# Moving five layer-1 modulation pieces of a two-layer hybrid kernel from the first mixer into the first expert stage

## The chip, the core and the metric

The kernel runs on one core of one Trainium2 chip. The metric is the device time of one execution in microseconds (us). The core has five instruction streams that run beside each other: TensorE (PE, matmuls), VectorE (DVE), ScalarE (ACT), GpSimd (POOL) and SyncE (SP). SP's queue issues nearly all transfers from memory; the core's 16 DMA engines carry them out.

## What is computed

Two layers over 256 tokens of width 1024. Each layer computes a modulation vector from the conditioning vector, uses six slices of it (shift, scale and gate, once for the mixer and once for the experts), and ends in a mixture of 16 experts. Cut to what matters:

```python
for layer in range(2):
    mod = silu(c) @ ada_w[layer] + ada_b[layer]        # 1024 x 6144 weights
    shift1, scale1, gate1, shift2, scale2, gate2 = split(mod, 6)
    h = rmsnorm(x, norm_mix[layer]) * (1 + scale1) + shift1
    mix = attention_and_recurrence(h) if layer == 0 else fnet(h)
    x = x + gate1 * mix
    h2 = rmsnorm(x, norm_ffn[layer]) * (1 + scale2) + shift2
    x = x + gate2 * grouped_moe(h2)                    # 16 experts, 1024 -> 512 -> 1024
```

In the kernel `ada_w[layer]` is cut into 12 pieces `(l, j)` of 512 columns, 2 MB each. Pieces `(1, 0)` and `(1, 1)` are layer 1's first shift, `(1, 2)` and `(1, 3)` its first scale; both are read only after the experts of layer 0. `(1, 6)` is half of layer 1's second shift, read later still.

## The kernel before, in words

All weights flow through 16 slots of 1 MB (`NSLOT`), in one fixed order. `Stream.pump` (L114 to L130) issues the next half of a piece as soon as a slot is free; SP's queue then waits for the last reader of that slot. So the order of the stream and the moments at which slots are given back set when each transfer starts.

The work goes through these stages, with times of the profiled execution:

- up to about 140 us: modulation of the first mixer, its first projections, the forward recurrence;
- 140 to 182 us: the value projection (`vp`, eight steps of 12 matmuls) beside the backward recurrence on DVE, ACT and POOL;
- 182 to 252 us: attention (16 units: scores `s`, softmax, transposes `pt`, weighted sums `av`) with the output projection `mix` interleaved;
- 252 to 278 us: norm, router, ranks, the gathering of the first four experts' tokens `xg`;
- 278 to 492 us: the experts of layer 0, eight pairs; for each pair the matmuls `g`, `u` (L1054), `dn` (L1091), and scatter and gather matmuls between them;
- 492 to 575 us: the second mixer (FNet), norm and router;
- 575 us to the end: the experts of layer 1.

Eleven modulation pieces (`ADA`, L30) are worked into the first mixer as a side task. `ada_ve` (L365 to L389) sums a piece on DVE: one `tensor_scalar` and seven `scalar_tensor_tensor` of 128x512 into the buffer `gva`, then four tiny PE products with ones (L386) add over the partitions, and a small DVE addition writes `modc`. `ada_step` (pieces 2, 3 and 9 of the list, `ON_PE`) does a piece with 32 PE products (L333) instead. The side task goes on by so many steps at each step of the projections (`W_K`, `W_Q`, `W_G`, `W_V`, `W_A`, `W_P`). `ORDER` (L37) says where the pieces stand in the stream: each `a` is the next of `ADA`, the capitals are projection weights, `p` and `o` the output projection's.

The order on PE in the expert stages is the order of the code (`manual_schedule`); elsewhere a scheduler places instructions on each engine by priority and by its own estimates, and each engine then keeps that order strictly. `W.used(k)` and `W.done(i)` give a slot back.

Of the kernel before, what the change touches and what calls it, by code (L numbers as in the profile page):

```python
# [13 lines left out]
ALU = mybir.AluOpType  # L14
# [12 lines left out]
PRI = 50  # L27
LOW = 60

ADA = [(0, 4), (0, 5), (0, 6), (0, 7), (0, 8), (0, 9), (1, 0), (1, 2), (1, 1), (1, 3), (1, 6)]  # L30
ON_PE = (2, 3, 9)

FILL0 = [[(0, 10), (0, 11)], [(1, 4), (1, 5)], []]
FILL1 = [[(1, 10), (1, 11)], [], []]
A1_LATE = [(1, j) for j in (7, 8, 9, 10, 11)]

ORDER = 'aaQBaaGaaaVpoaaaa'  # L37

EK = 'vgvgvggv'
EQ = 'vggvggvv'  # L40
# [106 lines left out]
def hybrid_layers(  # L147
# [22 lines left out]
    ve, ac, te, gp = nc.vector, nc.scalar, nc.tensor, nc.gpsimd  # L170
# [11 lines left out]
    def wps(name="w"):  # L182
        return ps.tile([128, 512], F32, tag="w", name=name, bufs=3)

    def gps(name="g"):
        return ps.tile([128, 512], F32, tag="g", name=name, bufs=1)

    def buf(name, tag, size, bufs):
        return data.tile([128, size], F32, tag=tag, name=name, bufs=bufs)
# [23 lines left out]
    st = Stream(nc, slots, NSLOT)  # L213

    def ada_item(l, j):
        return st.chunk(("a", l, j), ada_w[l, j])
# [4 lines left out]
    def exp_items(l):  # L221
        order = [(n, p) for p in range(NE // 2) for n in "gud"]
        if l == 1:
            order[-6:] = [(n, p) for ns in ("gu", "d") for p in (6, 7) for n in ns]
        r = []
        for n, p in order:
            pair = [st.chunk((n, l, e), {"g": moe_g, "u": moe_u, "d": moe_d}[n][l, e], n == "d")
                    for e in (2 * p, 2 * p + 1)]
            if (l, n, p) == (1, "d", 7):

                r += [(c, a // 512, slice(a % 512, a % 512 + b - a)) for a, b in zip(CUTS, CUTS[1:]) for c in pair]
            else:
                r += [(c, i) for i in range(2) for c in pair]
        return r

    WQ, WK, WV, WXB, WGB = range(5)
# [12 lines left out]
    ones = cst[:, 128:256]  # L249
# [52 lines left out]
    ada_b = [cols[:, 94:142], cols[:, 142:190]]  # L302

    sc32 = const.tile([128, 8, 32], F32, name="sc32")
# [13 lines left out]
    modc = [const.tile([128, 48], F32, name=f"modc{l}") for l in range(2)]  # L318
# [49 lines left out]
    def ada_ve(l, j):  # L368

        W = st.get(("a", l, j))  # L370
        while not W.ready(0):
            yield
        r = buf("gva", "gva", 512, 1)
        with tc.high_priority(-LOW):
            ve.tensor_scalar(r, W[:, 0], sc32[:, 0, 0:1], None, op0=ALU.mult)
        yield
        for k in range(1, 8):
            while k == 4 and not W.ready(1):
                yield
            with tc.high_priority(-LOW):  # L380
                ve.scalar_tensor_tensor(r, W[:, k], sc32[:, k, 0:1], r, op0=ALU.mult, op1=ALU.add)  # L381
            W.used(k)
            yield
        p = gps("gv")
        for q in range(4):
            te.matmul(out=p[:, q:q + 1], lhsT=r[:, q * 128:(q + 1) * 128], rhs=ones[:, 0:1], start=True, stop=True)  # L386
        yield
        c4 = slice(4 * j, 4 * j + 4)
        ve.tensor_tensor(modc[l][:, c4], p[:, 0:4], ada_b[l][:, c4], op=ALU.add)  # L389
        yield  # L390

    def split(dst_h, src, dst_l, eng):
# [125 lines left out]
    def rows(p, w, nt, k):  # L518

        for t in range(nt):  # L520
            c = slice(t * 128, (t + 1) * 128)
            mm3(p[t], (hH[k][:, c], hL[k][:, c]), w, k == 0, k == 7)
# [35 lines left out]
    for g in range(2):  # L558
# [3 lines left out]
             "o": [st.chunk(("wo", 1), w_out[1])], "p": [st.chunk(("wo", 0), w_out[0])]}  # L562
    ada = iter(ADA)
    for c in ORDER:
        st.add(named[c] if c in named else [ada_item(*next(ada))])
# [37 lines left out]
    def gemm(W, step, on):  # L603

        w = {k: split_w(W[:, k], ENG[on[k]]) for k in range(2)}
        for k in range(8):
            if k + 2 < 8:
                w[k + 2] = split_w(W[:, k + 2], ENG[on[k + 2]])
                W.used(k + 2)
            step(w.pop(k), k)  # L610
            yield
# [92 lines left out]
    scan = [Task(r.scan()) for r in rec]  # L704
    side = Task(*[(ada_step if i in ON_PE else ada_ve)(*a) for i, a in enumerate(ADA)])
    for n, _ in enumerate(gemm(st.get(("win", WK)), lambda w, k: rows(kp, w, 4, k), EK)):
# [180 lines left out]
    def moe(l, xn, store):  # L887
# [5 lines left out]
        for kk in range(4):  # L893
            p = wps("tp")
            for i in range(4):
                k = 2 * kk + i // 2
                at = te.transpose(p[:, i * 128:(i + 1) * 128], xn[:, i % 2, k * 128:(k + 1) * 128], ident)
            for i in range(2):
                k = 2 * kk + i
# [10 lines left out]
        for k in range(8):  # L910
            q = slice(32 * (k % 4), 32 * (k % 4) + 32)
# [104 lines left out]
        def half(i):  # L1016
            return slice(64 * i, 64 * i + 64)
# [28 lines left out]
        def up(p, xg):  # L1046

            i0 = 2 * (p % 2)
            gu = [wps("g"), wps("u")]
            for n, q in zip("gu", gu):  # L1050
                W = [st.get((n, l, 2 * p + i)) for i in range(2)]
                for k in range(8):
                    for i in range(2):
                        te.matmul(out=q[half(i), :], lhsT=xg[:, k, half(i0 + i)], rhs=W[i][:, k],  # L1054
                                  start=(k == 0), stop=(k == 7))
                    for i in range(2):
                        W[i].used(k)
            act = t2k("act")[:, 0:512]
            ac.activation(act, gu[0], AF.Silu)  # L1059
            ve.tensor_tensor(act, act, gu[1], op=ALU.mult)  # L1060
            w = gps("st")
            for tb in range(2):
                te.transpose(w[:, tb * 128:(tb + 1) * 128], sg_of[p // 2][:, tb * 256 + i0 * 64:tb * 256 + i0 * 64 + 128], ident)  # L1063
            gcol = tn([128, 1], "gcol", bufs=2)
            ve.reduce_sum(gcol, w[:, 0:256], axis=AX.X)  # L1065
            ST = t1k("ST").bitcast(F32R)
            ve.tensor_scalar(ST, w[:, 0:256], 0.0, None, op0=ALU.is_gt)
            return p, act, gcol, ST
# [9 lines left out]
        def down(p, aT, gcol, ST):  # L1078
            last = store and p == 7
            if last:  # L1080
                for i in range(4):
                    add_gated(yacc[i], gate, i // 2, slice(i % 2 * 512, i % 2 * 512 + 512), gp)
            yH = t4k("yH").bitcast(F32R)
            yL = t4k("yL").bitcast(F32R)
            W = [st.get(("d", l, 2 * p + i)) for i in range(2)]
            cuts = CUTS if last else HALVES
            for c in map(slice, cuts, cuts[1:]):
                dn = wps("dn")[:, 0:c.stop - c.start]
                for fc in range(4):
                    for i in range(2):  # L1090
                        te.matmul(out=dn[half(i), :], lhsT=aT[:, fc * 128 + 64 * i:fc * 128 + 64 * i + 64],  # L1091
                                  rhs=W[i][:, fc, c], start=(fc == 0), stop=(fc == 3))
                ac.activation(yH[:, c], dn, AF.Copy, scale=gcol)  # L1093
                ve.scalar_tensor_tensor(yL[:, c], dn, gcol, yH[:, c].bitcast(F32), op0=ALU.mult, op1=ALU.subtract)  # L1094
                if last:
                    finish(c, yH, yL, ST)
                if c.stop % 512 == 0:
                    for i in range(2):
                        W[i].done(c.start // 512)
            return p, yH, yL, ST  # L1100

        early = None
        with tc.manual_schedule(engines={mybir.EngineType.PE}):
            for p in range(8):
                if p == 2:
                    scatter(*pend)
                    pend = None
                    gate = gate_rows(l, 40)
                    overflow(l, ci, over, xh, xl, a2, b2, gate)
                u = early or up(p, xg)  # L1110
                if p == 0:
                    for f in fins:
                        f()


                ahead = store and p == 6
                if pend:
                    scatter(*pend, (0, 1) if ahead else (0,))
                if p < 6 and p % 2 == 0:
                    nxt = gather(p // 2 + 1)  # L1120
                if p < 6 and not pend:
                    xg_ = next(nxt)
                if ahead:
                    early = up(7, xg)
                act_t = transposed_act(u[1])
                if pend and not ahead:
                    scatter(*pend, (1,))
                    if p < 6:
                        xg_ = next(nxt)
                if p == 5 and l == 0:  # L1130
                    load_dft()
                pend = down(u[0], act_t, *u[2:])
                if p % 2 == 1 and p < 7:
                    xg = xg_
            if not store:
                scatter(*pend)
# [65 lines left out]
    for cb in range(8):  # L1202
        with tc.issue_after(last.ins):
            side()
        p = wps("f1")
# [10 lines left out]
    for gp2 in range(2):  # L1216
# [5 lines left out]
        for b in range(2):  # L1222
            k = dict(start=(b == 0), stop=(b == 1))
# [103 lines left out]
```

## Time and profile before

| | |
|---|---|
| median of three runs | 803.24 us (802.31 to 805.01) |
| the profiled execution | 804.33 us, of which 802.5 us lie between its first and last instruction |
| mean granted TensorE clock | 0.957 |
| bytes moved | 277.33 MB, mean 346 GB/s |
| PE busy | 712.6 us, 89% |
| DVE busy | 353.2 us, 44% |

The shares are means over stages with different limits. The page's picture in 40 slices and the table by stage below show where each engine is full; the slice rows have one digit or one number for each 20 us.

### The profile page before, as it was taken

How to read it: one execution, taken by the hardware profiler on the slowest of the kernel's cores; microseconds unless marked ns; L12 is line 12 of the kernel's file. 1: busy time of each engine (PE TensorE's matmuls, PEld its weight loads, DVE VectorE, ACT ScalarE, POOL GpSimd, SP SyncE). 2: the span in 40 equal slices, each digit the busy share in tenths (PEclk: the TensorE clock that was granted, in tenths of full speed). 3: DMA queues.
4: the chain of work that ended last, by engine and by line, in shares of the span. 5: the costliest groups of instructions: out<-in, count | busy, mean ns of one | idle time of the engine just before them, and what ended most of it. 6: DMA issues, size and time to landing. Idle time of an engine off the chain costs nothing. (4 is left out here: it accounts for less than half of the span.)

```text
span 802.5 us, 10368 instructions
## 1 busy us (share of the span) xinstructions
PE 712.6 (89%) x4080; PEld 388.7 (48%) x4080; DVE 353.2 (44%) x648; ACT 236.9 (30%) x420; POOL 125.2 (16%) x100
## 2 busy tenths in 40 slices
PE   3999869897998899799999996978699799999986
PEld 2676557674657534244344333656434344334333
DVE  3559798898875511111121105794421121112015
ACT  6246738554555310110111003434210110011000
POOL 1132561444111201000000001051201000000002
PEclk9999988897999899999999999999799999999999
DMA  8987467563887799999999999999199999999991
GB/s 278 360 331 294 169 262 263 212 261 125 342 325 287 291 354 421 418 414 422 419 423 420 420 421 421 421 409 367 60 423 421 401 423 421 421 423 419 422 376 63
DMA packets 53789, 277.33 MB, mean 346 GB/s; under 512 B 4898, under 2 KB 20832, under 8 KB 22496
## 3 DMA queue, kind: packets, MB, share of 16 engines
q1 hardware_dynamic: 53584, 276.47, 86.3%
q8 instruction: 36, 0.59, 0.3%
q14 instruction: 25, 0.20, 0.1%
q10 hardware_dynamic: 144, 0.07, 0.0%
HBM read 275.47 MB, written 1.05 MB: 345 GB/s over the span
## 5 line engine op out<-in xcount | busy, mean ns | idle before, releaser
L1054 PE MATMUL g<-slot,xg 128*64 128x512 f32 x512 | 116.2, 608 | 8.0 <-PEq L1142 8.0
L1091 PE MATMUL dn<-slot,aT 128*64 128x512 f32 (+1 forms) x544 | 115.7, 577 | 4.1 <-DVE aT L1075 4.1
L1054 PE MATMUL u<-slot,xg 128*64 128x512 f32 x512 | 113.7, 593 | 0.8 <-DMA slot<-in_moe_u_dram 0.8
L1060 DVE TENSOR_TENSOR act<-act,u 128x512 f32<-128x512 f32 x16 | 11.0, 687 | 191.2 <-PE u L1054 191.2
L395 POOL TENSOR_TENSOR wp<-slot,wp 128x512 fp32r<-128x512 f32 x41 | 60.3, 1480 | 155.9 <-ACT wp L394 145.9
L1054 PEld LDWEIGHTS g<-slot,xg 128*64 128x64 f32 x512 | 38.3, 140 | 82.0 <-issue 81.1
L1054 PEld LDWEIGHTS u<-slot,xg 128*64 128x64 f32 x512 | 38.8, 137 | 72.9 <-issue 70.9
L381 DVE SCALAR_TENSOR_TENSOR gva<-slot,sc,gva 128x512 f32<-128x512 f32 x77 | 72.6, 943 | 1.1
L1091 PEld LDWEIGHTS dn<-slot,aT 128*64 128x64 f32 x544 | 37.9, 138 | 70.6 <-issue 61.0
L1094 DVE SCALAR_TENSOR_TENSOR yL<-dn,gcol,yH 128x512 fp32r<-128x512 f32 (+1 forms) x34 | 24.5, 720 | 99.0 <-ACT yH L1093 90.8
L1093 ACT ACTIVATE yH<-dn,gcol 128x512 fp32r<-128x512 f32 (+1 forms) x34 | 22.5, 662 | 139.9 <-PE dn L1091 139.9
L1009 ACT ACTIVATE xg<-xg,modc,a 128x256 f32<-128x256 f32 x32 | 18.0, 564 | 136.4 <-PE xg L1000 136.4
L394 ACT ACTIVATE wp<-slot 128x512 fp32r<-128x512 f32 x72 | 43.8, 625 | 46.3 <-PE mix L409 15.8
L1011 POOL TENSOR_TENSOR SG<-S,gates 128x512 f32<-128x512 f32 x8 | 8.4, 1044 | 310.4 <-PE st L1063 302.0
L1059 ACT ACTIVATE act<-g 128x512 f32<-128x512 f32 x16 | 9.6, 597 | 121.0 <-PE g L1054 121.0
L333 PE MATMUL gv<-slot,sc 128*32 128x128 f32 x832 | 34.6, 297 | 6.5 <-DVE modc L350 3.7
L333 PEld LDWEIGHTS gv<-slot,sc 128*32 128x32 f32 x832 | 27.6, 119 | 13.3 <-DVE modc L350 3.9
L1000 PE MATMUL xg<-S,xh 128*128 128x256 f32 x128 | 28.4, 306 | 3.8 <-DVE S L988 2.6
L1007 DVE TENSOR_SCALAR xg<-xg,a,modc 128x256 f32<-128x256 f32 x32 | 17.4, 543 | 29.2 <-ACT xg L1009 29.2
L395 DVE TENSOR_TENSOR wp<-slot,wp 128x512 fp32r<-128x512 f32 x31 | 25.5, 826 | 8.0 <-ACT wp L394 7.3
L1000 PE MATMUL xg<-S,xl 128*128 128x256 f32 x128 | 27.4, 298 | 0.0
L1031 PE MATMUL ya<-yH,ST 128*128 128x512 f32 x60 | 26.4, 440 | 0.6 <-ACT yH L1093 0.2
(258 smaller groups left out, 1125.5 us busy)
## 6 DMA issues: line engine op xcount, KB each, us to landing
slot<-in_moe_g_dram SPq DMA_DIRECT2D x64, 1024.0 KB, 14.2
slot<-in_moe_u_dram SPq DMA_DIRECT2D x64, 1024.0 KB, 14.4
slot<-in_moe_d_dram SPq DMA_DIRECT2D x60, 1024.0 KB, 16.5
slot<-in_ada_w_dram SPq DMA_DIRECT2D x40, 1024.0 KB, 7.4
slot<-in_w_in_dram SPq DMA_DIRECT2D x8, 1024.0 KB, 8.3
slot<-in_ada_w_dram SPq DMA_DIRECT2D x12, 512.0 KB, 9.2
slot<-in_w_out_dram SPq DMA_DIRECT2D x4, 1024.0 KB, 4.9
slot<-in_fnet_w_dram SPq DMA_DIRECT2D x4, 1024.0 KB, 19.8
```

What stands on the lines that cost most here:

```text
L333: te.matmul(out=p[32 * q:32 * q + 32, 0:128], lhsT=sc32[:, k, :], rhs=W[:, k, c:c + 128], start=(k == 0), stop=(k == 7))
L381: ve.scalar_tensor_tensor(r, W[:, k], sc32[:, k, 0:1], r, op0=ALU.mult, op1=ALU.add)
L394: ac.activation(dst_h, src, AF.Copy)
L395: eng.tensor_tensor(dst_l, src, dst_h.bitcast(F32), op=ALU.subtract)
L1000: at_xg[0] = te.matmul(out=p[:, i * 256:(i + 1) * 256], lhsT=xx[:, tb, k * 128:(k + 1) * 128], rhs=S[:, tb * 256:(tb + 1) * 256], start=(n ...
L1007: ve.tensor_scalar(xg[:, k], pv, a2[:, k:k + 1], b2[:, k:k + 1], op0=ALU.mult, op1=ALU.add)
L1009: ac.activation(xg[:, k], pv, AF.Identity, scale=a2[:, k:k + 1], bias=b2[:, k:k + 1])
L1031: te.matmul(out=yacc[tb * 2 + h], lhsT=ST[:, tb * 128:(tb + 1) * 128], rhs=y[:, h * 512:(h + 1) * 512], start=(p == 0 and n == 0), stop=(n ...
L1054: te.matmul(out=q[half(i), :], lhsT=xg[:, k, half(i0 + i)], rhs=W[i][:, k], start=(k == 0), stop=(k == 7))
L1091: te.matmul(out=dn[half(i), :], lhsT=aT[:, fc * 128 + 64 * i:fc * 128 + 64 * i + 64], rhs=W[i][:, fc, c], start=(fc == 0), stop=(fc == 3))
L1093: ac.activation(yH[:, c], dn, AF.Copy, scale=gcol)
L1094: ve.scalar_tensor_tensor(yL[:, c], dn, gcol, yH[:, c].bitcast(F32), op0=ALU.mult, op1=ALU.subtract)
```

## The change

`ADA` loses its five pieces of layer 1, `ON_PE` its entry for the one of them that was on PE, and `ORDER` the five places for them. In the stream of layer 0's experts each of the first five pairs is now followed by one of these pieces (`exp_items`). A new generator `ada_inplace` sums a piece on DVE with the same eight instructions, but into the piece's own first slot instead of `gva`. It is started behind the pair's `down`; its four small PE products and its addition follow behind the next pair's `up`. The summed slot is given back only then.

```diff
-ADA = [(0, 4), (0, 5), (0, 6), (0, 7), (0, 8), (0, 9), (1, 0), (1, 2), (1, 1), (1, 3), (1, 6)]
-ON_PE = (2, 3, 9)
+ADA = [(0, 4), (0, 5), (0, 6), (0, 7), (0, 8), (0, 9)]
+ON_PE = (2, 3)
+
+A1_EARLY = [(1, 0), (1, 2), (1, 1), (1, 3), (1, 6)]
...
-ORDER = 'aaQBaaGaaaVpoaaaa'
+ORDER = 'aaQBaaGaVpoa'
...
                 r += [(c, i) for i in range(2) for c in pair]
+            if l == 0 and n == "d" and p < len(A1_EARLY):
+                r.append(ada_item(*A1_EARLY[p]))
...
+    def ada_inplace(l, j):
+
+        W = st.get(("a", l, j))
+        r = W[:, 0]
+        ve.tensor_scalar(r, r, sc32[:, 0, 0:1], None, op0=ALU.mult)
+        for k in range(1, 8):
+            ve.scalar_tensor_tensor(r, W[:, k], sc32[:, k, 0:1], r, op0=ALU.mult, op1=ALU.add)
+        W.done(1)
+        yield
+        p = wps("gv")
+        for q in range(4):
+            te.matmul(out=p[:, q:q + 1], lhsT=r[:, q * 128:(q + 1) * 128], rhs=ones[:, 0:1], start=True, stop=True)
+        c4 = slice(4 * j, 4 * j + 4)
+        ve.tensor_tensor(modc[l][:, c4], p[:, 0:4], ada_b[l][:, c4], op=ALU.add)
+        W.done(0)
+        yield
...
                 u = early or up(p, xg)
+                if l == 0 and 0 < p <= len(A1_EARLY):
+                    next(ada)
...
                 pend = down(u[0], act_t, *u[2:])
+                if l == 0 and p < len(A1_EARLY):
+                    ada = ada_inplace(*A1_EARLY[p])
+                    next(ada)
```

DVE's queue at the start of attention, before the change: `mx` and `P` belong to the softmax, `wp` to the output projection, `gva` to the side task's pieces `(1, 2)` and `(1, 1)`.

```order
L776 TENSOR_REDUCE mx<-s 128x1
L774 TENSOR_TENSOR s<-s,bg 128x256
L395 TENSOR_TENSOR wp<-slot_1330,wp 128x512
L776 TENSOR_REDUCE mx<-s 128x1
L381 SCALAR_TENSOR_TENSOR gva<-slot_1379,sc_127,gva 128x512
L784 RECIPROCAL sm<-sm 128x1
L774 TENSOR_TENSOR s<-s,bg 128x256
L785 TENSOR_SCALAR P<-P,sm 128x512
L389 TENSOR_TENSOR modc_141<-gv,cols 128x4
L375 TENSOR_SCALAR gva<-slot_1412,sc_127 128x512
L776 TENSOR_REDUCE mx<-s 128x1
L381 SCALAR_TENSOR_TENSOR gva<-slot_1412,sc_127,gva 128x512
```

The same place in the changed kernel, from the last instruction of the recurrence (`yl`) on:

```order
L718 TENSOR_TENSOR yl<-yl,A 128x256 x2
L416 TENSOR_TENSOR wp<-slot_1182,wp 128x512
L436 SCALAR_TENSOR_TENSOR a_0_2068<-modc_140,cols 128x8
L795 TENSOR_TENSOR s<-s,bg 128x256 x2
L797 TENSOR_REDUCE mx<-s 128x1 x2
L795 TENSOR_TENSOR s<-s,bg 128x256
L797 TENSOR_REDUCE mx<-s 128x1
L805 RECIPROCAL sm<-sm 128x1
L806 TENSOR_SCALAR P<-P,sm 128x512
```

The sums into `gva` are gone from between the softmax instructions; nothing else has come in their place.

DVE's queue in the second expert pair, before: `aT` is what the pair's `dn` matmuls read, `yL` follows `dn`.

```order
L1065 TENSOR_REDUCE gcol<-st 128x1
L1067 TENSOR_SCALAR ST<-st 128x256
L1075 COPY aT<-at 128x512
L1007 TENSOR_SCALAR xg<-xg,a_0_2185,modc_140 128x256 x2
L1094 SCALAR_TENSOR_TENSOR yL<-dn,gcol,yH 128x512 x2
```

And now; `slot_2501` and `slot_2503` are the two halves of piece `(1, 2)`, and `modc_141` is layer 1's modulation.

```order
L1088 TENSOR_SCALAR ST<-st 128x256
L409 TENSOR_TENSOR modc_141<-gv,cols 128x4
L400 TENSOR_SCALAR slot_2501<-slot_2501,sc_127 128x512
L402 SCALAR_TENSOR_TENSOR slot_2501<-slot_2501,sc_127 128x512
L1096 COPY aT<-at 128x512
L402 SCALAR_TENSOR_TENSOR slot_2501<-slot_2501,sc_127 128x512 x2
L1028 TENSOR_SCALAR xg<-xg,a_0_2068,modc_140 128x256
L402 SCALAR_TENSOR_TENSOR slot_2501<-slot_2503,sc_127,slot_2501 128x512
L1028 TENSOR_SCALAR xg<-xg,a_0_2068,modc_140 128x256
L402 SCALAR_TENSOR_TENSOR slot_2501<-slot_2503,sc_127,slot_2501 128x512 x3
L1115 SCALAR_TENSOR_TENSOR yL<-dn,gcol,yH 128x512 x2
```

The scheduler has put the first two sums of the piece ahead of the pair's own `aT` copy, the rest ahead of `yL`.

SP's queue behind piece `(0, 8)` (slots 937 and 948), before:

```order
L130 DMA slot_937<-in_ada_w_dram 128x2048
L130 DMA slot_948<-in_ada_w_dram 128x2048
L130 DMA slot_995<-in_ada_w_dram 128x2048
L130 DMA slot_1013<-in_ada_w_dram 128x2048
L130 DMA slot_1139<-in_ada_w_dram 128x2048
L130 DMA slot_1157<-in_ada_w_dram 128x2048
L130 DMA slot_1182<-in_w_in_dram 128x2048
L130 DMA slot_1214<-in_w_in_dram 128x2048
```

And now:

```order
L132 DMA slot_937<-in_ada_w_dram 128x2048
L132 DMA slot_948<-in_ada_w_dram 128x2048
L132 DMA slot_995<-in_w_in_dram 128x2048
L132 DMA slot_1013<-in_w_in_dram 128x2048
L132 DMA slot_1139<-in_w_out_dram 128x2048
L132 DMA slot_1157<-in_w_out_dram 128x2048
L132 DMA slot_1182<-in_w_out_dram 128x2048
L132 DMA slot_1214<-in_w_out_dram 128x2048
L132 DMA slot_1243<-in_ada_w_dram 128x2048
L132 DMA slot_1284<-in_ada_w_dram 128x2048
```

The value weights (`w_in`) have moved up by four places, and piece `(0, 9)`, which followed `(0, 8)` directly (slots 995 and 1013 of before), now stands behind the output projection's weights (slots 1243 and 1284 of the changed kernel).

## Rows read from the trace of the kernel before

**Rows 1.** The page: span, and what DMA moved, one entry per 20 us.
```profile
span 802.5 us, 10368 instructions
...
GB/s 278 360 331 294 169 262 263 212 261 125 342 325 287 291 354 421 418 414 422 419 423 420 420 421 421 421 409 367 60 423 421 401 423 421 421 423 419 422 376 63
```

**Rows 2.** Busy time by stage, with granted clock, DMA share and rate.
```profile
core 0: us, PE busy (x) PEld busy (x) DVE busy (x) ACT busy (x) POOL busy (x), PEclk, DMA share, GB/s
...
140.00:182.00 42.00, 37.40 (x170) 29.43 (x169) 38.15 (x47) 23.74 (x36) 19.49 (x13) 0.88 0.59 226
182.00:202.00 20.00, 14.76 (x48) 10.09 (x50) 16.28 (x27) 9.47 (x21) 9.60 (x9) 0.74 0.44 154
202.00:252.00 50.00, 48.05 (x331) 32.83 (x331) 36.53 (x82) 26.79 (x58) 7.53 (x5) 1.00 0.80 314
...
278.00:492.00 214.00, 204.31 (x974) 83.74 (x974) 36.59 (x64) 23.91 (x39) 6.93 (x5) 0.99 0.99 408
```

**Rows 3.** PE's waits in the experts of layer 0: total us, times, longest.
```profile
PE u L1054 <- DMA slot<-in_moe_u_dram: 0.8, 1, 0.8
```

**Rows 4.** PE's timeline at the last pair: start, us, instruction, idle before.
```profile
477.78 3.65 PE L1054 MATMUL u<-slot,xg 128*64 128x512 f32 x14 [0.77 <-DMA slot<-in_moe_u_dram]
...
484.53 7.09 PE L1091 MATMUL dn<-slot,aT 128*64 128x512 f32 x32
```

**Rows 5.** SP's timeline around the start of the experts: transfers issued.
```profile
265.38 4.22 SPq L130 DMA_DIRECT2D slot<-in_moe_g_dram  x4
281.56 4.36 SPq L130 DMA_DIRECT2D slot<-in_moe_u_dram  x4
```

**Rows 6.** SP's timeline at the end of layer 0's experts.
```profile
460.40 7.78 SPq L130 DMA_DIRECT2D slot<-in_moe_d_dram  x4
470.34 7.78 SPq L130 DMA_DIRECT2D slot<-in_fnet_w_dram  x4
```

**Rows 7.** Transfers issued by L130, 440 to 480 us.
```profile
DMA to landing us min/median/max: 18.0/19.8/19.9
```

**Rows 8.** The page: DMA issues, count, KB each, median us to landing.
```profile
slot<-in_ada_w_dram SPq DMA_DIRECT2D x40, 1024.0 KB, 7.4
```

**Rows 9.** Groups on PE, 139.5 to 252 us: count, busy us, mean ns.
```profile
L386 PE MATMUL gv<-cst,gva 128*128 128x1 f32 x40 | 6.8, 291 | 5.2 <-DVE gva L381 4.7 <-DVE catL L395 0.3
...
L333 PE MATMUL gv<-slot,sc 128*32 128x128 f32 x68 | 2.3, 276 | 0.0
```

**Rows 10.** PE's waits, 140 to 252 us.
```profile
PE gv L386 <- DVE gva L381: 4.7, 3, 3.0
PE s L767 <- ACT P L779: 4.7, 2, 3.4
PE mix L409 <- POOL catL L395: 1.1, 1, 1.1
PE mix L407 <- ACT v L745: 0.6, 1, 0.6
```

**Rows 11.** The piece sums on DVE, 140 to 250 us: ns min/median/max.
```profile
L381 DVE SCALAR_TENSOR_TENSOR gva<-slot,sc,gva x34: 726/744/1783, 140.0 to 229.3; 128x512 f32<-128x512 f32 x34
```

**Rows 12.** DVE's timeline where PE waits for the softmax.
```profile
189.66 0.42 DVE L774 TENSOR_TENSOR s<-s,bg 128x256 f32<-128x256 f32 x1
190.00 0.88 DVE L381 SCALAR_TENSOR_TENSOR gva<-slot,sc,gva 128x512 f32<-128x512 f32 x1
190.79 0.68 DVE L776 TENSOR_REDUCE mx<-s 128x1 f32<-128x512 f32 x1
```

**Rows 13.** The chain that ended last, in order of time: start, us, what.
```profile
712.64 6.87 PE g L1054 x32
...
738.51 6.87 PE g L1054 x32
...
771.45 8.68 PE dn L1091 x32
```

## The prediction

> **What bounds the kernel now.** I read the page's slices first, then busy time by stage, then PE's waits stage by stage, and last SP's timeline, which tells when transfers could start.
>
> The slices show two kinds of stage. From 300 us on the DMA engines are full at about 420 GB/s, except around 560 to 580 us (60 GB/s) and in the tail; before 300 us they move between 125 and 360 GB/s [rows 1]. So bytes are cheap in the first mixer and dear in the expert stages.
>
> In the first mixer the limit is a mixture. From 140 to 252 us PE is busy 37.40 of 42, 14.76 of 20 and 48.05 of 50 us, at granted clocks 0.88, 0.74 and 1.00, while DVE is busy 38.15 of 42, 16.28 of 20 and 36.53 of 50 us [rows 2]. PE's waits there end with the piece sums (4.7 us), with the softmax (4.7 us) and with the recurrence's results (1.7 us), never with a DMA [rows 10]. The softmax wait is DVE's too: a score tile is finished at 191.5 us because sums into `gva` stand before and between its two instructions [rows 12].
>
> The experts of layer 0 are at both limits at once. DMA is 99% busy and PE 204.31 of 214 us [rows 2]. PE waits for a transfer only once, 0.77 us before the last pair's `u` [rows 3, 4]. But that wait matters: the prefetch of 16 slots has been used up exactly there. The last `down` half is issued at 467.9 us (460.40 plus 7.78, less the 0.3 us that an issue takes) [rows 6]; with the 19.8 us that transfers of this time took to land [rows 7] it is there at 487.7 us, and PE's second half of `dn` wants it at 484.53 + 3.55 = 488.1 us [rows 4]. There is 0.4 us of slack at the end of this stage.
>
> **What the change adds.** Five pieces are ten transfers of 1024 KB, 10.49 MB [rows 8]. At 420 GB/s [rows 1] that is 25.0 us, now in a stage that has next to none to spare. The prefetch cannot take it up: before the first `g` all 16 slots already hold experts. SP issues the second pair's `g` at 265.38 us and the next transfer only at 281.56 us, after the first `g` gave slots back [rows 5]. In the changed kernel the slots will be just as full, with one `ada` piece among them. So the last `down` lands 25.0 us later, counted from the first `g`, and PE ends the stage that much later. Bounds: 0 if something I don't see lets DMA catch up, and 25.7 at the stage's mean of 408 GB/s [rows 2]. I take 25.0, since the transfers come where the rate is 420.
>
> [...]
>
> Behind this stage nothing changes: the second mixer is paced by compute, the transfers it needs stand behind the last `down` in the same order as now [rows 6], and the DMA engines idle near 570 us with all slots full in both kernels [rows 1]. So the 25 us are not won back in layer 1.
>
> The forty DVE sums move along. Median 744 ns each [rows 11], they are 30 us in a stage where DVE is busy 36.59 of 214 us [rows 2]: hidden. If that cover failed, because two of them now stand ahead of an `aT` copy, it is a rival below. The PE products with ones (6.8/5 = 1.4 us a piece [rows 9], 7 us in all) fall into PE's new waits for DMA: nothing; without those waits they would cost their 7 us. PE will wait 25 us in this stage, so part of it runs cold. A `dn` that starts after a wait took 8.68 us, a warm one 7.09 [rows 13, 4]; the last pair is exposed to that once: 1.6 us. Its bounds are 0 and a whole cold tail, which the rival on PE prices.
>
> **What the change takes from the first mixer.** Everything up to place 47 of SP's queue is unchanged, so the gain starts after about 140 us. Three terms, for 140 to 252 us:
>
> - PE instructions that go. Four of the five DVE pieces of this stretch (32 of 40 products): 6.8 x 32/40 = 5.4 us; the piece on PE: 2.3 x 64/68 = 2.2 us [rows 9]. Together 7.6 us, fairly certain.
> - PE's waits. PE is idle 4.60 + 5.24 + 1.95 = 11.8 us [rows 2]. Of these I give back 8: 3.7 of the 4.7 behind `gva` (piece `(0, 9)` remains and can be waited for once), 4.3 of the 4.7 behind the softmax, none of the 1.7 behind the recurrence [rows 10].
> - The clock. 42 x 0.12 + 20 x 0.26 = 10.2 us are lost to the low level [rows 2], all next to waits. If three quarters of the waits go, I take half of it: 5.1 us.
>
> That is 20.7 us. Against it, the first piece's sums now stand between the evacuations of the first gathered tokens, just before the first `g`: five sums, 3.7 us; the evacuations also wait for PE's matmuls there, so I charge a fifth, 0.7 (all of it would be 3 us more, which the range holds). Gain: 20 us. Bounds: at most 7.6 + 11.8 + 10.2 = 29.6 us, if PE never waits and is never cold; at least 7.6 less 3.0, the longest present wait for a sum [rows 10], in case `(0, 9)`, which now is loaded behind the output projection's weights, comes late: 4.6 us.
>
> [...]
>
> **The sum.** The profiled execution took 804.33 us, span 802.5. 804.33 - 20 + 25.0 + 1.6 = 810.9 us; it stood 1.1 us above the median of the runs, so I forecast 810 us, 0.8% slower. Its own range, with the gain between 14 and 24 us, is 806 to 816.
>
> **Rivals.**
>
> *The mixer gives back everything* (the one that ends on the other side). If DVE alone sets the pace from 140 us to the middle of attention, then without the sums the value projection runs warm and attention starts at once: 29.6 us gained against 25.0, 799 us. For it: DVE at 91% of 140 to 182 us, and the sums just ahead of the softmax. Against it: 202 to 252 us PE is busy 96% at full clock, so there only the 3 to 4 us of removed products can be had, and the recurrence on DVE, ACT and POOL stays. It decides from a gain of 26.6 us on; between that and 24 us the change is lost in the noise. Chance 0.20.
>
> *Only the removed PE instructions count.* The waits move on to the recurrence or to `(0, 9)`, the clock stays low: 7.6 us, 804.33 - 7.6 + 26.6 - 1.1 = 822 us. For it: the recurrence's chain runs through three engines and keeps all its instructions. Against it: the softmax wait is plainly behind sums. Chance 0.15.
>
> *The bytes are hidden.* The expert stage is paced by PE (204 of 214 us), DMA only looks full: 804.33 - 20 - 1.1 = 783 us. Against it: the 0.77 us wait at the end and 488.1 against 487.7 us. Chance 0.03.
>
> *PE loses more than the bytes in the expert stage.* DVE's queue is strict, and at the second pair `aT` waits behind a sum that waits for a piece loaded after this pair's `down`: two transfers, 5 us, at each of five pairs 25 us; or PE, cold by waiting, needs more than a pair's transfer time. 810 + 25 = 835 us at most. Against it: PE needs what comes next in the stream anyway, which lands later still, and a pair's 26 us of PE (`g` recurs after 25.9 us in layer 1 [rows 13]) have 30 to 35 us of transfers beside them. Chance 0.04.
>
> [...]
>
> **How the numbers follow.** Forecast 0.58, rivals 0.20, 0.15, 0.03, 0.04. A measurement of this kernel tells about 0.3% (2.4 us) from no change. Faster by more: 0.08 from the first rival and 0.03 from the third, 0.11. Within: 0.12 from the first and 0.08 from the forecast's low edge, 0.20. Slower: 0.69. The range that holds 8 in 10 is 801 to 820 us: it takes in half of the first rival and the better part of the second.
>
> **What would show it.** In the changed profile the first `g` starts near 258 us instead of 278; 300 to 500 us stays at 420 GB/s; PE waits some 20 to 25 us for `slot` transfers in the later pairs of layer 0, where it waited 0.8; layer 0's experts last about 240 us instead of 214; the second mixer and layer 1 keep their lengths. I am wrong if the expert stage keeps its 214 us, if the first `g` comes before 252 us, or if DVE's sums, not DMA, end PE's waits there.

## The result and the profile after

| | before | after |
|---|---|---|
| median | 802.87 us (802.31 to 805.01, 4 runs) | 816.12 us (812.92 to 818.29, 4 runs) |
| ratio | | 1.0158, 95% interval 1.0129 to 1.0187 |
| profiled execution | 804.33 us, span 802.5 | 812.92 us, span 811.1 |
| first `g` of layer 0 | 277.88 us | 256.72 us |
| experts of layer 0, first `g` to end of last `dn` | 213.7 us | 244.5 us |
| second mixer, to layer 1's first `g` | 83.4 us | 83.0 us |
| layer 1's first `g` to the end of the span | 227.5 us | 226.9 us |

The change costs about 13 us, 1.6%. The forecast was 810 us with a range of 801 to 820: the direction and the range hold, but the loss is 6 us larger than forecast. In the two profiled executions the mixer gives 21.2 us, the experts of layer 0 take 30.8 us, and the rest is 0.4 and 0.6 us shorter: +8.6 us. The medians are 13.2 us apart. The profiled execution of the changed kernel was its fastest, with a mean granted clock of 0.954 where the other three runs had 0.950; 0.004 of 811 us is 3.2 us, which has the size of the difference. But the three runs at 0.950 lie 2.5 us apart (815.75 to 818.29), so the clock does not explain it all; they have no trace, and where they lost the time stays open.

The page of the changed kernel: span and what DMA moved, one number for each 20 us, as in [rows 1].

```profile
span 811.1 us, 10265 instructions
...
GB/s 286 362 334 286 168 240 311 120 311 149 156 309 243 427 419 421 247 424 421 421 421 420 421 422 421 421 421 377 99 396 421 416 379 421 421 421 422 421 386 96
```

The full stretch begins at 264 us instead of 301, and it has a hole: 247 GB/s in the 17th slice (324 to 345 us), where [rows 1] has 409 to 423 from the 16th to the 27th. No step of the prediction has that hole.

Busy time by stage after the change; columns as in [rows 2].

```profile
140.00:182.00 42.00, 37.56 (x175) 28.30 (x173) 37.10 (x48) 29.48 (x48) 25.69 (x20) 0.96 0.61 227
182.00:231.00 49.00, 48.59 (x279) 33.29 (x281) 30.91 (x71) 28.88 (x65) 8.32 (x6) 1.00 0.46 167
140.00:231.00 91.00, 86.15 (x452) 61.60 (x454) 68.01 (x118) 58.35 (x110) 34.01 (x26) 0.98 0.53 195
320.00:340.00 20.00, 6.38 (x24) 2.35 (x26) 6.35 (x9) 0.00 (x0) 0.00 (x0) 0.59 0.67 256
```

The first three rows are the gain. The stretch that took 112 us now ends 21 us earlier, at 231 us. PE was busy 37.40 + 14.76 + 48.05 = 100.2 us there [rows 2] and is busy 86.15 us now; it was idle 11.8 us and is idle 4.85 us. The granted clock of 0.88 and 0.74 [rows 2] has become 0.96 and 1.00. The last row is the loss: in 320 to 340 us PE works 6.38 us of 20, at a granted clock of 0.59.

PE's waits from 140 to 231 us after the change (total us, times, longest), beside [rows 10].

```profile
PE gv L390 <- DVE gva L385: 2.3, 1, 2.3
PE mix L428 <- ACT v L766: 1.5, 1, 1.5
PE mix L430 <- POOL catL L416: 0.6, 1, 0.6
PE s L788 <- ACT P L800: 0.3, 1, 0.3
```

The softmax wait fell from 4.7 to 0.3 us and that for `gva` from 4.7 to 2.3 us; the recurrence's results are waited for 2.1 us instead of 1.7.

The products of the side task that are left from 139.5 to 231 us, beside [rows 9]: count, busy us, mean ns.

```profile
L390 PE MATMUL gv<-cst,gva 128*128 128x1 f32 x8 | 1.1, 253 | 2.3 <-DVE gva L385 2.3
L337 PE MATMUL gv<-slot,sc 128*32 128x128 f32 x13 | 0.6, 280 | 0.0
```

They went from 6.8 + 2.3 us to 1.1 + 0.6 us: 7.4 us.

SP's timeline at the start of the experts, beside [rows 5].

```profile
260.39 0.80 SPq L132 DMA_DIRECT2D slot<-in_moe_g_dram  x2
263.83 4.24 SPq L132 DMA_DIRECT2D slot<-in_moe_u_dram  x4
```

As before, SP goes on 3.7 us after the first `g` has begun (260.39 - 256.72; 281.56 - 277.88): the slots were full.

PE's waits in the experts of layer 0 (257 to 502 us), beside [rows 3].

```profile
PE g L1075 <- DVEq L1168: 21.5, 1, 21.5
PE u L1075 <- DMA slot<-in_moe_u_dram: 6.9, 6, 1.3
PE g L1075 <- DMA slot<-in_moe_g_dram: 1.9, 2, 1.3
```

The waits for transfers are there, but they are 8.8 us in eight pieces where 20 to 25 us were forecast. The largest wait is another: 21.5 us at once, released by DVE's sequencer at L1168. That line is the overflow branch (`tc.If(n > CAP)` in `overflow`), which all engines pass at the start of the third pair.

DVE's queue just ahead of that branch, in the order of its instructions (`slot_2650` and `slot_2652` are the halves of the third piece, `(1, 1)`):

```
L1115 SCALAR_TENSOR_TENSOR yL<-dn,gcol,yH 128x512 x2
L400 TENSOR_SCALAR slot_2650<-slot_2650,sc_127 128x512
L402 SCALAR_TENSOR_TENSOR slot_2650<-slot_2650,sc_127 128x512 x3
L402 SCALAR_TENSOR_TENSOR slot_2650<-slot_2652,sc_127,slot_2650 128x512 x2
L1167 TENSOR_LOAD ci
L1168 COMPARE_AND_BRANCH
```

In the code this piece's sums stand behind the third pair's `down`, so behind the branch. The scheduler drew six of its eight sums ahead of it. Three timelines show what that does (start, us, instruction, idle before and its releaser). DVE:

```profile
308.18 0.75 DVE L1115 SCALAR_TENSOR_TENSOR yL<-dn,gcol,yH 128x512 fp32r<-128x512 f32 x1 [2.48 <-ACT yH L1114]
326.18 0.49 DVE L400 TENSOR_SCALAR slot<-slot,sc 128x512 f32<-128x512 f32 x1 [17.25 <-DMA slot<-in_ada_w_dram]
326.70 2.33 DVE L402 SCALAR_TENSOR_TENSOR slot<-slot,sc 128x512 f32<-128x512 f32 x3
329.06 1.54 DVE L402 SCALAR_TENSOR_TENSOR slot<-slot,sc,slot 128x512 f32<-128x512 f32 x2
333.45 1.54 DVE L402 SCALAR_TENSOR_TENSOR slot<-slot,sc,slot 128x512 f32<-128x512 f32 x2 [2.85 <-DVEq L1168]
```

PE:

```profile
310.26 1.88 PE L449 MATMUL gb<-dg,cst 128*128 128x512 f32 x4
333.62 8.47 PE L1075 MATMUL g<-slot,xg 128*64 128x512 f32 x32 [21.48 <-DVEq L1168]
```

SP, which issues the transfers:

```profile
307.41 1.76 SPq L132 DMA_DIRECT2D slot<-in_ada_w_dram  x2
311.33 0.33 SPq L132 DMA_DIRECT2D slot<-in_moe_g_dram  x1
335.02 7.41 SPq L132 DMA_DIRECT2D slot<-in_moe_g_dram  x4
```

What SP waited for at 335.02 us and behind it, and how long transfers issued from 300 to 313 us took to land:

```profile
SPq L132 <- DVE slot L402: 6.3, 1, 6.3
SPq L132 <- PE g L1075: 5.9, 2, 3.3
DMA to landing us min/median/max: 17.3/19.0/19.8
```

The piece is issued at 307.4 us and its first half lands at about 326 us. DVE stands still for it for 17.25 us. PE has come to the branch at 312 us and goes on at 333.6 us, when DVE has passed it. SP comes to the branch after one more transfer and issues nothing until 335.02 us, a pause of 23.4 us: in its queue one `g` stands between the piece and the branch, four behind it. The branch is not all that holds SP. The slot that it fills at 335.02 us is given back by the last of the piece's own sums, which ends at 334.99 us behind the branch, and two of the next by PE's `g`. So as long as PE stands at the branch, none of its matmuls reads a slot and gives it back. What is queued lasts some 17 to 20 us, and then the DMA engines run out of work. What they moved from 300 to 345 us, in 40 slices of 1.1 us:

```profile
DMA  9999999999999999999999999820000099888999
GB/s 393 422 422 408 444 415 401 459 386 430 430 415 422 393 415 459 386 422 437 393 437 415 422 444 386 357 117 0 7 0 22 0 160 430 342 124 364 444 408 430
```

The slices from 357 on fall short of 420 GB/s by 3127 in sum (63, 303, 420, 413, 420, 398, 420, 260, 0, 78, 296, 56); 3127 x 1.125 us / 420 = 8.4 us of transfers not made, in a stage that is paced by transfers.

The last pair of layer 0, beside [rows 4]:

```profile
487.35 3.65 PE L1075 MATMUL u<-slot,xg 128*64 128x512 f32 x14 [1.31 <-DMA slot<-in_moe_u_dram]
...
494.10 7.09 PE L1112 MATMUL dn<-slot,aT 128*64 128x512 f32 x32
```

The last `u` is waited for 1.31 us instead of 0.77. The `dn` behind it takes 7.09 us, as before: no cold tail. Layer 1 has the chain of [rows 13] again, shifted: its `g` are 25.87 us apart.

```profile
722.77 6.87 PE g L1075 x32
...
748.64 6.87 PE g L1075 x32
```

### The profile page after: what moved, and what is told of

Read it like the earlier page. It is cut to its first block, busy times and chain, and to the rows that moved or that the text cites. A ratio compares the mean times of both kernels' runs of the same rounds, so it can differ in the third digit from the quotient of the medians.

```text
span 811.1 us, 10265 instructions
## 1 busy us (share of the span) xinstructions
PE 703.9 (87%) x4023; PEld 381.4 (47%) x4023; DVE 358.4 (44%) x656; ACT 236.3 (29%) x419; POOL 123.5 (15%) x100
## 5 line engine op out<-in xcount | busy, mean ns | idle before, releaser
L1075 PE MATMUL g<-slot,xg 128*64 128x512 f32 x512 | 118.5, 607 | 27.6 <-DVEq L1168 21.5
L1075 PE MATMUL u<-slot,xg 128*64 128x512 f32 x512 | 116.9, 593 | 6.9 <-DMA slot<-in_moe_u_dram 6.9
L385 DVE SCALAR_TENSOR_TENSOR gva<-slot,sc,gva 128x512 f32<-128x512 f32 x49 | 45.4, 926 | 0.9
L337 PE MATMUL gv<-slot,sc 128*32 128x128 f32 x768 | 32.6, 299 | 7.4 <-DVE modc L354 5.2
L337 PEld LDWEIGHTS gv<-slot,sc 128*32 128x32 f32 x768 | 25.9, 120 | 13.8 <-DVE modc L354 5.4
L1028 DVE TENSOR_SCALAR xg<-xg,a,modc 128x256 f32<-128x256 f32 x32 | 17.3, 541 | 23.5 <-ACT xg L1030 23.5
## 6 DMA issues: line engine op xcount, KB each, us to landing
slot<-in_moe_d_dram SPq DMA_DIRECT2D x60, 1024.0 KB, 17.3
slot<-in_ada_w_dram SPq DMA_DIRECT2D x40, 1024.0 KB, 10.1
slot<-in_fnet_w_dram SPq DMA_DIRECT2D x4, 1024.0 KB, 19.8
```

The costliest lines, as they stand in the source:

```text
L337: te.matmul(out=p[32 * q:32 * q + 32, 0:128], lhsT=sc32[:, k, :], rhs=W[:, k, c:c + 128], start=(k == 0), stop=(k == 7))
L1028: ve.tensor_scalar(xg[:, k], pv, a2[:, k:k + 1], b2[:, k:k + 1], op0=ALU.mult, op1=ALU.add)
```

## The experiments

The theory from these rows: the change takes some 20 us off the first mixer and brings 25 us of bytes, as predicted, and the rest is the empty stretch at the branch, some 8 us. The rivals: the sums or PE's waits in the expert stage cost it, or the bytes cost more than their rate says. The ratios are to runs of the kernel before on the same chip.

| run | median us (range, runs) | ratio to before, 95% interval | first `g` | experts of layer 0 |
|---|---|---|---|---|
| after | 816.12 (812.92 to 818.29, 4) | 1.0158 (1.0129 to 1.0187) | 256.7 | 244.5 |
| e1_skip_third | 808.09 (804.88 to 811.79, 7) | 1.0062 (1.0037 to 1.0086) | 257.4 | 237.2 |
| e2_bytes_only | 807.91 (806.72 to 812.15, 5) | 1.0053 (1.0034 to 1.0073) | 260.9 | 237.3 |
| e3_pieces_gone | 783.05 (781.35 to 785.78, 4) | 0.9750 (0.9724 to 0.9776) | 256.5 | 212.3 |
| e4_pieces_on_pe | 806.36 (801.69 to 808.90, 9) | 1.0041 (1.0018 to 1.0063) | 280.0 | 213.4 |
| e5_order_only | 801.78 (799.57 to 806.98, 12) | 1.0002 (0.9978 to 1.0026) | 275.1 | 213.0 |
| e6_order_and_pe | 798.51 (793.88 to 801.11, 12) | 0.9948 (0.9925 to 0.9971) | 269.3 | 212.4 |
| e7_late_shift | 799.89 (796.15 to 800.83, 12) | 0.9961 (0.9943 to 0.9978) | 269.3 | 214.4 |
| e8_no_branch | 802.87 (801.73 to 807.00, 10) | 1.0005 (0.9983 to 1.0026) | 256.9 | 235.6 |
| e9_before_no_branch | 797.32 (795.89 to 799.68, 6) | 0.9922 (0.9902 to 0.9941) | 277.9 | 212.0 |

The medians of before were 803.22 us (16 runs) beside e1 to e4, 803.52 (35 runs) beside e5 to e8 and 803.60 (11 runs) beside e9.

### e1: no piece ahead of the branch

```diff
-A1_EARLY = [(1, 0), (1, 2), (1, 1), (1, 3), (1, 6)]
+A1_EARLY = {0: (1, 0), 1: (1, 2), 3: (1, 1), 4: (1, 3), 5: (1, 6)}
...
-            if l == 0 and n == "d" and p < len(A1_EARLY):
+            if l == 0 and n == "d" and p in A1_EARLY:
...
-                if l == 0 and 0 < p <= len(A1_EARLY):
+                if l == 0 and p - 1 in A1_EARLY:
...
-                if l == 0 and p < len(A1_EARLY):
+                if l == 0 and p in A1_EARLY:
```

The same five pieces; the third follows the fourth pair instead of the third.

> The changed kernel, but the third piece stands behind the fourth pair instead of the third (pieces behind pairs 0, 1, 3, 4, 5), so that none of its sums stands in DVE's queue ahead of the branch of the overflow code. Bytes and sums are the same. Theory (the excess over the forecast is a bubble: DVE waits 17 us for the third piece ahead of the branch, all engines meet at the branch, SP cannot issue, DMA runs empty for about 8 us): DMA stays at 420 GB/s from 300 to 340 us, PE's wait at the branch is back to about 4 us, the experts of layer 0 last 236 to 239 us instead of 244.5, and the time falls by 6 to 10 us to 806 to 811. Rival (the bytes alone set the end of the stage, the wait at the branch only came earlier than it would have come): time within 2 us of the changed kernel, 814 to 818, with the same sum of PE waits spread over later pairs.

Measured 808.09 us, 8.0 us below the changed kernel, as the theory had it. The stretch of the hole (columns as in [rows 2]) and SP's timeline there:

```profile
320.00:340.00 20.00, 18.23 (x98) 8.03 (x96) 3.11 (x7) 1.73 (x3) 0.00 (x0) 1.00 1.01 420
```

```profile
308.04 4.25 SPq L132 DMA_DIRECT2D slot<-in_moe_g_dram  x3
323.12 0.34 SPq L132 DMA_DIRECT2D slot<-in_moe_g_dram  x1
```

420 GB/s instead of 256, and the experts of layer 0 are 7.3 us shorter. PE is idle at the branch for 3.97 us. SP pauses here too, for 10.8 us (308.04 + 4.25 to 323.12), but that is shorter than the 17.3 to 19.8 us that queued transfers took to land in the changed kernel, and the DMA engines stay full. The number of pieces, their bytes, sums and products are the same, so it is the place of one piece that costs 8 us.

### e2: the bytes without the sums

As e1, and the eight sums and four products of a piece are replaced by two small additions that read the slots:

```diff
-        r = W[:, 0]
-        ve.tensor_scalar(r, r, sc32[:, 0, 0:1], None, op0=ALU.mult)
-        for k in range(1, 8):
-            ve.scalar_tensor_tensor(r, W[:, k], sc32[:, k, 0:1], r, op0=ALU.mult, op1=ALU.add)
+        c4 = slice(4 * j, 4 * j + 4)
+        ve.tensor_tensor(modc[l][:, c4], W[:, 4, 0:4], ada_b[l][:, c4], op=ALU.add)
...
-        p = wps("gv")
-        for q in range(4):
-            te.matmul(out=p[:, q:q + 1], lhsT=r[:, q * 128:(q + 1) * 128], rhs=ones[:, 0:1], start=True, stop=True)
-        c4 = slice(4 * j, 4 * j + 4)
-        ve.tensor_tensor(modc[l][:, c4], p[:, 0:4], ada_b[l][:, c4], op=ALU.add)
+        ve.tensor_tensor(modc[l][:, c4], W[:, 0, 0:4], modc[l][:, c4], op=ALU.add)
```

> As e1_skip_third, but the eight sums and the four products of each moved piece are left out: the five pieces are still loaded, two additions of 128x4 read them (so layer 1's modulation from these pieces is left out). Theory (the sums are hidden, only the bytes cost): within 2 us of e1_skip_third. Rival (the sums in DVE's queue or their products on PE delay the experts): 5 to 10 us below e1_skip_third.

Measured 807.91 us, 0.2 us from e1, and the experts take 237.3 us against 237.2. Forty DVE sums and twenty products cost nothing beyond the noise, some 2.5 us by the two intervals. (Its first `g` at 260.9 us is of a profile that was the longest of its five runs.)

### e3: the pieces gone

The five pieces are neither loaded nor summed:

```diff
-            if l == 0 and n == "d" and p < len(A1_EARLY):
-                r.append(ada_item(*A1_EARLY[p]))
...
-        ve.tensor_tensor(modc[l][:, c4], p[:, 0:4], ada_b[l][:, c4], op=ALU.add)
+        ve.tensor_copy(modc[l][:, c4], ada_b[l][:, c4])
```

> The changed kernel with the five pieces neither loaded nor summed (layer 1's modulation from these pieces is left out). It shows what the first mixer gives back by itself. Theory: first g near 256.7 us, experts of layer 0 back to 214 us, time 780 to 784, so that e1_skip_third lies 25 us above it: 10.49 MB at 420 GB/s. Rival (part of the loss is not bytes): e1_skip_third lies 30 us or more above it; other rival (part of the bytes is hidden): 20 us or less.

Measured 783.05 us: 20.2 us below before, which is the mixer's gain by itself, since the expert stage has its old length to 1.4 us (212.3 after 213.7). And e1 is 808.09 - 783.05 = 25.0 us above it; its expert stage is 237.2 - 212.3 = 24.9 us longer. That is the price of 10.49 MB at 420 GB/s, 25.0 us; by the two intervals the difference of the medians is known to some 3 us.

### e4 to e7: what of the mixer's gain is to be had without moving bytes

These start from the kernel before. e4 puts all five pieces on PE, so that DVE loses their sums:

```diff
-ON_PE = (2, 3, 9)
+ON_PE = (2, 3, 6, 7, 8, 9, 10)
```

> The kernel before, with the five layer-1 pieces left where they are in the stream of the first mixer, but all of them as 32 PE products each instead of sums on DVE. Theory (the first mixer's gain is DVE's relief, and its bytes cost nothing there): first g at 258 to 266 us, experts of layer 0 at 214 us, time 785 to 793, faster than both kernels. Rival (the gain of the first mixer came from fewer bytes and from earlier value weights): first g at 274 to 280, time 799 to 805.

Measured 806.36 us, 0.4% slower than before. Three stretches of it (columns as in [rows 2]) and PE's waits from 140 to 252 us:

```profile
140.00:182.00 42.00, 33.09 (x262) 25.78 (x261) 34.52 (x37) 21.68 (x36) 24.52 (x18) 0.90 0.54 201
182.00:202.00 20.00, 20.00 (x211) 13.35 (x210) 7.47 (x19) 8.02 (x17) 3.12 (x4) 0.87 0.60 209
202.00:252.00 50.00, 49.59 (x301) 34.06 (x300) 29.16 (x67) 28.52 (x63) 8.32 (x6) 1.00 0.78 307
```

```profile
PE gv L340 <- ACT gvr L339: 5.9, 1, 5.9
PE gv L386 <- DVE gva L381: 3.0, 1, 3.0
```

DVE is relieved as meant (7.47 of 20 us where [rows 2] has 16.28) and PE hardly waits for the softmax any more (0.2 us). But PE is idle 8.9 us of the first 42 instead of 4.60, now behind ACT's step of the PE pieces, and after that it is full. I had expected 785 to 793 us, and the rival 799 to 805: both were too low. Taking the sums off DVE gives nothing where PE has to do the pieces instead: its busy time in the three stretches is 102.7 us, where it was 100.2.

e5 leaves the pieces as they are and moves only the value and output weights up in the stream:

```diff
-ORDER = 'aaQBaaGaaaVpoaaaa'
+ORDER = 'aaQBaaGaVpoaaaaaa'
```

> The kernel before with all eleven pieces in the first mixer as they were (DVE and PE), but the stream in the changed kernel's order as far as it can be: value and output weights directly behind the first piece after the gate weights (ORDER 'aaQBaaGaVpoaaaaaa'), so piece (0, 9) and all of layer 1 come behind them. Theory A (part of the mixer's gain is that PE no longer stands 3 us before the value projection waiting for the sum of piece (0, 9), and then runs cold): the value projection starts near 146 us instead of 152, first g 4 to 8 us earlier, time 795 to 799. Theory B (the gain is the removed sums alone): first g within 2 us of 278, time 801 to 805.

Measured 801.78 us, not to be told from before and in theory B's range; the first `g` comes 2.8 us earlier in the profile, between the two theories. e6 has both edits.

> e5_order_only with, besides, all five layer-1 pieces as PE products instead of sums on DVE. If in e4_pieces_on_pe the relief of DVE was eaten by the wait for piece (0, 9) and the cold stretch behind it, which this order takes away, first g comes at 264 to 270 us and the time is 789 to 795. If it was eaten by the PE products themselves (about 2 us a piece beside the 1.4 us they replace) and their ACT copies, first g is at 272 or later and the time 797 or more.

Measured 798.51 us, 0.5% below before: the lowest median here of a kernel that computes the whole. The time is that of the second case, the first `g` at 269.3 us that of the first; but the profile is of its fastest run, 793.88 us, 4.6 us below the median. PE's waits from 140 to 252 us, the two longest:

```profile
PE gv L333 <- DVE modc L350: 3.5, 1, 3.5
PE gv L386 <- DVE gva L381: 2.4, 1, 2.4
```

In that profile the first `g` comes 8.6 us earlier than before, where the change has 21. By the medians e6 gains 5.0 us where e3 gains 20.2. The rest was not had without taking the pieces out of the mixer. From 140 to 252 us its PE is busy 103.25 us, 3.0 more than before, with the pieces' products. The two edits give more together than the sum of each: with the order alone PE waits 6.3 us for `gva`, with the pieces alone 5.9 us for `gvr`.

e7 takes e6 and moves `(1, 6)` into the second mixer, to the pieces of `A1_LATE`:

```diff
-ON_PE = (2, 3, 6, 7, 8, 9, 10)
+ON_PE = (2, 3, 6, 7, 8, 9)
-A1_LATE = [(1, j) for j in (7, 8, 9, 10, 11)]
+A1_LATE = [(1, j) for j in (6, 7, 8, 9, 10, 11)]
-ORDER = 'aaQBaaGaVpoaaaaaa'
+ORDER = 'aaQBaaGaVpoaaaaa'
```

> e6_order_and_pe with piece (1, 6), which is read only by the experts of layer 1, loaded and summed in the second mixer with its neighbours (1, 7) to (1, 9), where DMA idles some 16 us at the end. If the idle time there takes its 5 us of transfer and DVE its 6 us of sums: 2 to 3 us below e6_order_and_pe. If the second mixer is paced by DVE: the second mixer grows by up to 6 us and the time is 0 to 5 us above e6_order_and_pe.

Measured 799.89 us, with an interval that covers e6. In the profiles the second mixer took 86.6 us against 84.1, which points to the second case, that the piece's work is not free there either; with one profile of each, and e6's of its fastest run, that is not settled.

### e8 and e9: both kernels without the branch

e8 is the changed kernel, e9 the kernel before, each without this line, for both layers:

```diff
-                    overflow(l, ci, over, xh, xl, a2, b2, gate)
```

> The changed kernel with the branch to the overflow code left out in both layers (that code runs only when an expert has more than 64 tokens); the third piece keeps its place in the stream behind the third pair. Theory (it is the meeting of all engines at the branch that lets DMA run empty): no bubble near 330 us, layer 0's experts 235 to 239 us, time 800 to 808 (the branch itself also costs about 4 us in layer 1). Rival (the third piece's place in the stream costs the time): layer 0's experts stay at 243 us or more, time 810 or more.

> The kernel before, with the overflow branch left out of both layers (its code and the load of the count that it tests). It is the partner of the run that left the branch out of the changed kernel, 802.87 us: the difference of the two is the change without a meeting at the branch. In the profile of before PE waits 4.1 us at the branch in layer 0 and 3.9 us in layer 1. Theory (the bubble is a meeting of engines at the branch that only the changed kernel pays dearly; the branch alone costs its 3.9 us in layer 1, where PE sets the pace, and little in layer 0, where transfers end last): 799.5 us, 798 to 801, so that the change alone costs 802.87 - 799.5 = 3 to 5 us, the 25 us of bytes less the 20 of the mixer. Rival A (the branch costs its full wait in both layers of before): 795.5 us, so that the change alone costs 7 us and the bubble explains only some 6. Rival B (the branch costs nothing where it is met without waiting): 803.5 us, and the change alone would cost nothing, so that all 13 us would be the branch's.

e8 measured 802.87 us. The third piece stands at its old place in the stream (its issue is the first row), but its sums are no longer drawn forward: they follow the third pair's first `yL`. SP goes on:

```profile
307.62 1.66 SPq L132 DMA_DIRECT2D slot<-in_ada_w_dram  x2
311.44 8.27 SPq L132 DMA_DIRECT2D slot<-in_moe_g_dram  x4
321.36 7.78 SPq L132 DMA_DIRECT2D slot<-in_moe_u_dram  x4
```

```profile
320.00:340.00 20.00, 19.15 (x104) 8.51 (x102) 5.66 (x11) 2.53 (x5) 0.00 (x0) 1.00 1.02 422
```

Its experts of layer 0 take 235.6 us, 8.9 less than in the changed kernel. Since the order of the sums changed together with the branch, e8 does not tell what a waiting sum would cost there without a branch behind it. e9 measured 797.32 us, 2 us below what I had expected and about as far above rival A: leaving the branch out of the kernel before is worth 1.7 us in layer 0's experts and 4.7 us from layer 1's first `g` on. So the total of e8 may not be set against before with its branch. Pair against pair, the change costs 1.58% with the branch and 1.0005 / 0.9922 - 1 = 0.84% without it; 0.74%, 5.9 us, is what the branch makes of it. By the two intervals that is known to some 3 us, and e1's 7.7 us (1.0158 - 1.0062) lies within. The pair gives 0.84%, 6.7 us, for the change without a meeting, which is rival A's 7 us rather than the theory's 3 to 5; e1 gives 808.09 - 803.22 = 4.9 us for it, which is the theory's. Within the 3 us the runs do not decide between the two.

## Why the prediction was right in direction and short by 6 us

Three differences of medians split the time up: before 803.22, less 20.2 for the mixer (e3), plus 25.0 for the bytes (e1 less e3), plus 8.0 for the hole at the branch (after less e1), is 816 us. They close by construction, so the sum proves nothing; each term has a check of its own: 21.2 us in the profiles for the mixer, 10.49 MB at 420 GB/s for the bytes, 8.4 us of transfers not made and 5.9 us from e8 and e9 for the hole. The forecast had 20, 25.0, nothing, and 1.6 us for a cold tail: it is 6 us short because the 8.0 us were missing and the 1.6 us did not come.

The direction is not luck: without the hole (e1) the kernel is 0.6% slower than before, where 0.8% was forecast. That 816 us still lies in the range is luck in part: its upper end stood there for the rival with 822 us, not for a hole.

- *The mixer's gain*, forecast 20 us: right, 21.2 us in the profile and 20.2 us in e3. Its terms: removed products 7.6 forecast, 7.4 measured. Waits 8 forecast, 11.8 - 4.85 = 6.9 measured; they went where I had said for the softmax (4.7 to 0.3), less so for `gva` (4.7 to 2.3). The clock 5.1 forecast; PE's busy time fell by 100.2 - 86.15 = 14.1 us, of which the products are 7.4, so 6.7 us are left, which I put down to running at the higher level (0.96 and 1.00, where it was 0.88 and 0.74). The 0.7 us charged for the sums ahead of the first `g` did not show: from the end of the compared stretch to the first `g` it takes 25.7 us, and took 25.9.
- *The bytes*, 25.0 us: right, within the 3 us to which it was measured. The step that made it possible, that the slots are full before the first `g` and that 0.4 us of slack is no cover, holds: with e1's order nothing of the 25 us is seen to be hidden, and the rival by which the bytes are hidden falls.
- *"The forty DVE sums move along ... hidden"* and, in the list of what would show, *"300 to 500 us stays at 420 GB/s"*: this is the step that failed. The sums' time is hidden (e2), but a sum that waits holds DVE's queue (17.25 us here), and I followed that only to the `aT` copies. The line for it in the rival on PE's loss was right about the strictness and wrong about the place: not a PE instruction behind `aT`, but the branch at the third pair, at which PE and SP stand as well. Against that rival I had argued that PE needs what comes next in the stream anyway, and that it lands later still. That holds while PE has loaded slots to read; at the branch it stood for 21.5 us with loaded slots that it could not read, and so gave none back. One of the signs that I had named for being wrong, *"if DVE's sums, not DMA, end PE's waits there"*, came true for the largest wait. The order of the changed kernel had `slot_2650` ahead of the branch for all to see; I read the second pair and not the third.
- *The cold tail*, 1.6 us: did not occur. The last `dn` took 7.09 us. The term rested on one `dn` of layer 1 that took 8.68 us, after a wait of 0.85 us and at a granted clock of 0.82; in the same trace the `dn` at 295.25 us also starts after a wait, of 0.78 us, and takes 7.09, at a granted clock of 1.00, so that a wait of that length alone does not make a `dn` cold. PE's waits for transfers are 1.3 us at the longest, and the granted clock of 460 to 502 us was 1.00.
- *PE's 20 to 25 us of waits for transfers*: not so, even without the hole. In e1 they are 10.1 us; of the 23.5 us by which its expert stage is longer than before, PE is busy for 10.8 us (214.88 instead of 204.05), with twenty products more, and idle for the rest.
- *The stages behind*: right. Second mixer 83.0 after 83.4 us, layer 1 within 0.6 us.
- *The first rival*, that the mixer gives back everything, needed 26.6 us and got 20 to 21. e4 points to why: DVE is not alone in setting the pace there. *The second*, that only removed products count, falls with the first `g` at 256.7 us.

The forecast counted 1.1 us for the profile's place among its runs; here the changed kernel's profile stood 3.2 us below its median, the other way round. A single profile stands some us from its median to either side, and the term was not worth a sentence.

## What to carry to other kernels

A wait that is hidden on one engine is hidden only up to the next place where all engines meet: here DVE waited 17.25 us for one transfer, and PE stood 21.5 us at the branch, where it had stood 4.1. Before work with its own transfer is put on an idle engine, look for runtime branches and other meeting points behind it in that engine's queue, in the order that the scheduler made and not in the code, and ask which engine still gives buffers back meanwhile, and for how long the transfers already queued last. Work that moves from a stage paced by compute into one where DMA is full costs its bytes at the stage's rate (10.49 MB at 420 GB/s, 25.0 us here, known to some 3 us); the gain elsewhere must be larger than that.

## What the runs showed of the hardware

Passing a branch whose body is not run costs PE more than I had thought: in the kernel before 4.1 us of idle time in layer 0 and 3.8 us in layer 1 (the first row below, PE's wait there; the releaser is PE's own sequencer). Without the branch (e9) layer 1 is 4.7 us shorter in the profile. The time lies in PE's branch instruction itself: it lasts 6.09 to 6.19 us there and 6.09 to 6.14 us in the changed kernel, and it begins while PE's last matmuls still run (at 330.5 and 627.4 us, where the last four begin at 331.05 and 628.21). Those of DVE, SP, ACT and POOL last 45 to 72 ns. (The two rows after it: duration in ns, shortest, median, longest; PEld is the queue of PE's weight loads.)

```profile
PE g L1054 <- PEq L1142: 3.8, 1, 3.8
```

```profile
L1142 PEldq COMPARE_BRANCH  x2: 6092/6140/6188, 330.5 to 627.4; - x2
L1142 DVEq COMPARE_BRANCH  x2: 63/68/72, 329.6 to 626.6; - x2
```

No run here shows what takes the 6 us, nor why PE alone pays it.

In layer 0, where transfers end last, the branch costs less than in layer 1: e9 without it is 1.7 us shorter there.
